# Three GpSimd products of the SSD scan issued on VectorE, in a hybrid SSD and S5 decoder step

## The chip, the cores and the metric

The kernel runs on one core of a Trainium2 chip. The metric is the device time of one execution in microseconds. The kernel before takes 1764.91 us (median of three runs, 1763.91 to 1765.38). In the names below, TensorE is PE, VectorE is DVE, ScalarE is ACT, GpSimd is POOL, and SyncE, whose queue issues all transfers here, is SP.

## The reference

One layer with two token mixers works on 1024 prompt tokens and on 64 tokens of 8 sample sequences, 1088 in all. One projection of the normed input (w_in, 1024 to 10272 columns) gives the columns of both mixers. The part that the change touches is the first mixer, a Mamba-2 scan in chunks of 128 tokens, with 32 heads of 64 columns in 8 groups of 4 heads:

```python
X = x.astype(jnp.float32) * dt[..., None]
dA = dt * A
A_cs = jnp.cumsum(dA, axis=-1)
Lmat = jnp.exp(jnp.where(causal, A_cs[..., :, None] - A_cs[..., None, :], -jnp.inf))
CB = jnp.einsum('bclgn,bcsgn->bgcls', Cc, Bc)
Y_diag = jnp.einsum('bgcls,bgrcls,bcsgrp->bclgrp', CB, Lmat, X)
decay_states = jnp.exp(A_cs[..., -1:] - A_cs)
states = jnp.einsum('bclgn,bgrcl,bclgrp->bcgrpn', Bc, decay_states, X)
...
Y_off = jnp.einsum('bclgn,bcgrpn,bgrcl->bclgrp', Cc, new_states[:, :-1], jnp.exp(A_cs))
Y = Y_diag + Y_off
```

So a chunk needs X (x times dt), X times decay_states for the state that it adds, and C times exp(A_cs) for what it takes from the state before it.

## The kernel before

Weights stand on TensorE as the fixed operand, and tokens stream. A product in float32 is made of three: the weight tile is split into a rounded part, `whi` (ACT, L143), and a rest, `wlo` (DVE, L144), the input is split likewise (`hh`, `hl`), and `dense` (L146) issues for each of 8 slices whi by hh, wlo by hh, whi by hl. A weight tile of 128 columns is used in three blocks of 512, 288 and 288 tokens, that is 24 matmuls each. `raw`, `whi` and `wlo` have two buffers each, so a tile can be split while the tile before it is in use.

The scan runs in eight stages, one for each group of heads. A main stream issues the tiles of group g+1 (`conv_tile`: three tap products on DVE at L591, a tanh on ACT at L592, L593 on DVE; `gate_tile`: tanh L606, product L607), and `drive` (L161) lets a side stream, `ssd` of group g, step in after each block; the table BESIDE says how many steps stand behind each block. `ssd` first handles the sample tokens (chunk 8) and then, for c from 0 to 7, `prepare(c+1)` and `outputs(c)`.

`prepare` loads the cumulated decays (`bca`, an SP transfer, two buffers), has PE transpose x and B into PSUM (`pst`), and then makes: the mask (`msk`: L671 on DVE, four exponentials on ACT at L673, L682 on DVE), B's split (`b`, `bt`), `xdt` (x times dt, DVE from PSUM, L679), `xd` (xdt times the decay, POOL, L681), C times exp(A_cs) in place of `bca` (exponential on ACT at L684, product on POOL at L685), and the split of `xd` (rounded part by ACT at L688, rest `xl` on POOL at L689). `outputs` multiplies msk by xdt and bca by the state `st` into `psy`, DVE writes the sum with the skip term from it (`ysb`, L743), PE makes the chunk's state in `pss`, and DVE forms the new state: the old one times the chunk's decay (L752), plus `pss` (L753). `st` is needed by the next chunk's matmuls.

Engines run their own instructions in order. The framework's scheduler sets the order on DVE, ACT, POOL and SP when the program is built; on PE the order is that in which the code issues the matmuls (class `Ordered`). `decays` (L483) makes the factors for all chunks once, ahead of the stages: `dt`, `dec` and others, each a tile of 9 times 32 columns.

Of the kernel before, what the change touches and what calls it, by code (L numbers as in the profile page):

```python
# [12 lines left out]
F32 = mybir.dt.float32  # L13
# [4 lines left out]
MUL, ADD, SUB, MAX, MIN = ALU.mult, ALU.add, ALU.subtract, ALU.max, ALU.min  # L18

P = 128  # L20
# [53 lines left out]
class Kernel:  # L74
# [408 lines left out]
    def decays(self, p):  # L483

        nc, pk, cn = self.nc, self.pk, self.cn
        V, S = nc.vector, nc.scalar
# [32 lines left out]
        ea = self.t(p, [P, 256], "xdt", 2)[:, :32]  # L519
# [41 lines left out]
        V.tensor_tensor(self.dec[:64, 256:], tots[:64, :32], self.ncs[:64, 256:], op=ADD)  # L561
        S.activation(self.dec[:, :256], self.dec[:, :256], AF.Exp)
        S.activation(self.dec[:64, 256:], self.dec[:64, 256:], AF.Exp)
        ts = self.psum("s")
        self.mm(ts[:, :256], self.ones[:64], dab.rearrange("p b h -> p (b h)"), start=True, stop=True)
        S.activation(self.etots, ts[:, :256], AF.Exp)
# [65 lines left out]
    def ssd(self, p, g, xcs, szs):  # L632

        nc, a = self.nc, self.a
        V, S, G = nc.vector, nc.scalar, nc.gpsimd
# [8 lines left out]
        h4 = lambda x: x.rearrange("p (h q) -> p h q", h=4)  # L644
# [4 lines left out]
        def prepare(c):  # L649
            smp = c == 8  # L650
            L = 64 if smp else P
            hc = c * 32 + 4 * g
            cl = slice(c * P, c * P + L)
            ea = self.t(p, [P, 4, L], "bca", 2)
            nc.sync.dma_start(ea, self.d["cs"][4 * g:4 * g + 4, cl].partition_broadcast(P))
            if smp:
                xs = []
                for src in (x0, x1, Bc, Cc):
                    d = self.t(p, [P, 64], "xsm", 4)
                    G.tensor_copy(d.rearrange("p (b t) -> p b t", t=8),  # L660
                                  src[:, 1027:].rearrange("p (b t) -> p b t", t=11)[:, :, :8])
                    xs.append(d)
            else:
                xs = [s[:, cl] for s in (x0, x1, Bc, Cc)]
            pt = self.psum("t")
            for j in range(3):
                self.tr(pt[:L, j * P:(j + 1) * P], xs[j], self.ident)
            self.mm(pt[:L, 384:384 + L], xs[2], xs[3], start=True, stop=True)
            m = self.t(p, [P, 4, L], "msk", 2)
            ng = self.cn[:64, C_SNEG:C_SNEG + 64] if smp else self.neg  # L670
            V.tensor_tensor(m[:L], ea[:L], ng.unsqueeze(1).to_broadcast([L, 4, L]), op=ADD)  # L671
            for h in range(4):
                S.activation(m[:L, h], m[:L, h], AF.Exp, bias=self.ncs[:L, hc + h:hc + h + 1])  # L673
            bt = None if smp else (self.t(p, [P, P], "b3", 2, F32R), self.t(p, [P, P], "bt", 2, F32R))
            if not smp:
                S.copy(bt[0], pt[:, 256:384])
                V.tensor_tensor(bt[1], pt[:, 256:384], bt[0].bitcast(F32), op=SUB)
            xdt = self.t(p, [P, 256], "xdt", 2)
            V.tensor_tensor(h4(xdt[:L]), h4(pt[:L, :256]), self.dt[:L, hc:hc + 4].unsqueeze(2).to_broadcast([L, 4, 64]), op=MUL)  # L679
            xd = self.t(p, [P, 256], "xd", 1)  # L680
            G.tensor_tensor(h4(xd[:L]), h4(xdt[:L]), self.dec[:L, hc:hc + 4].unsqueeze(2).to_broadcast([L, 4, 64]), op=MUL)  # L681
            V.tensor_tensor(m[:L], m[:L], pt[:L, 384:384 + L].unsqueeze(1).to_broadcast([L, 4, L]), op=MUL)  # L682
            if 0 < c < 8:
                S.activation(ea, ea, AF.Exp)  # L684
                G.tensor_tensor(ea, ea, xs[3].unsqueeze(1).to_broadcast([P, 4, L]), op=MUL)  # L685
            if not smp:
                xh, xl = self.t(p, [P, 256], "x3", 2, F32R), self.t(p, [P, 256], "xl", 2, F32R)
                S.copy(xh, xd)  # L688
                G.tensor_tensor(xl, xd, xh.bitcast(F32), op=SUB)  # L689
                xd = xh, xl  # L690
            bx = smp and [stack(h, pt[:, 256:384], xd) for h in range(2)]
            chunk[c] = (L, hc, cl, xs, ea, m, bt, xdt, xd, bx)

        def stack(h, bs, xd):


            own, other, last = (slice(32 * q, 32 * q + 32) for q in (h, 1 - h, 2))
            b3, x3 = self.t(p, [P, P], "b3", 2, F32R)[:96], self.t(p, [P, 256], "x3", 2, F32R)[:96]
            S.copy(b3[own], bs[own])
            S.copy(b3[last], bs[own])  # L700
            V.tensor_tensor(b3[other], bs[own], b3[own].bitcast(F32), op=SUB)
            S.copy(x3[own], xd[own])
            S.copy(x3[other], xd[own])
            V.tensor_tensor(x3[last], xd[own], x3[own].bitcast(F32), op=SUB)
            bx = self.t(p, [96, 4, P], "bx", 2, F32R)
            V.tensor_tensor(bx, b3.bitcast(F32).unsqueeze(1).to_broadcast([96, 4, P]),
                            self.cn[:96, C_S3:C_S3 + 4].unsqueeze(2).to_broadcast([96, 4, P]), op=MUL)
            return bx, x3
# [50 lines left out]
        def round_(r):  # L759
            bx, x3 = chunk[8][-1][r]  # L760
            for tag, b in ((("s", 0), ("t", 2)), (("y", 0), ("y", 2)))[r]:
# [4 lines left out]
                V.tensor_tensor(sv, sv, sp, op=ADD)  # L766

        prepare(8)
        yield
        past = earlier()  # L770
# [9 lines left out]
        nc.sync.dma_start(a["ssm_s"][g], s0)  # L780
        self.s0 = load(g + 1) if g < 7 else None
        prepare(0)
        yield
        for c in range(8):
            if c < 7:
                prepare(c + 1)
                yield
            outputs(c)
            yield
# [771 lines left out]
```

## Time and profile before

| | |
|---|---|
| median of three runs | 1764.91 us (1763.91 to 1765.38) |
| the profiled execution | 1763.57 us |
| its span, first to last instruction | 1761.4 us |
| mean granted TensorE clock | 0.994 |
| busy: PE, DVE, ACT, POOL | 1719.2, 1176.7, 685.4, 425.1 us |
| the eight scan stages | about 474 to 1215 us of the span |

A row of a timeline has the start in us, the length in us, the engine, the line, the operation, the tile written and the tiles read with buffer numbers left out, and in brackets how long the engine stood idle before it and for whom it waited. Instructions of one engine overlap a little: the next may start up to 0.09 us before the end that is recorded for the one ahead of it. A row of windows has, for a stretch of time, the busy time of each engine with the number of instructions in brackets, and then the clock that TensorE was granted.

### The profile page before, as it was taken

What the parts mean: (1) busy time and instruction counts of PE and PEld (TensorE: products, weight loads), DVE (VectorE), ACT (ScalarE), POOL (GpSimd) and SP (SyncE); (2) the same over time, 40 slices, a digit from 0 to 9 for tenths busy, and PEclk for the clock granted to TensorE, in tenths of its full rate; (3) what the DMA queues carried; (4) which work ended last, traced back from release to release, by engine and by line L of the source; (5) the groups of instructions that cost most, each with busy time, mean ns of one, the idle gap of its engine ahead of it and who ended that gap; (6) DMA issues with size and microseconds to landing.
All of it is one profiled execution on the core that took longest, in us unless ns stands there. A gap on an engine that the chain in (4) does not pass through costs nothing.

```text
span 1761.4 us, 31495 instructions
## 1 busy us (share of the span) xinstructions
PE 1719.2 (98%) x12510; PEld 1559.5 (89%) x12510; DVE 1176.7 (67%) x1976; ACT 685.4 (39%) x1414; POOL 425.1 (24%) x588
## 2 busy tenths in 40 slices
PE   9999999999999999999999999999999999999996
PEld 8997888889888888888878888888899989999996
DVE  6899977636586777778676877754565723485444
ACT  6422222223354544545444445445632302242221
POOL 0013212100143333424243333332341000022014
PEclk9999999999999999999999999999999999999998
DMA  5334343442132223232332222334523855474522
GB/s 209 96 103 117 103 152 106 126 143 76 54 105 91 91 79 121 62 126 61 87 107 80 100 89 96 108 117 147 165 98 122 259 175 195 132 226 137 197 97 75
DMA packets 138690, 212.62 MB, mean 121 GB/s; under 512 B 14832, under 2 KB 95120, under 8 KB 136496
## 3 DMA queue, kind: packets, MB, share of 16 engines
q1 hardware_dynamic: 138544, 210.62, 37.3%
q8 instruction: 98, 1.61, 0.4%
q14 instruction: 48, 0.39, 0.1%
HBM read 158.55 MB, written 52.03 MB: 120 GB/s over the span
## 4 chain that ended last, share of the span: by engine, by line
PE 70%; DVE 14%; DMA 5%; ACT 5%; issue 3%; POOL 2%; SPq 0%; POOLq 0%; ACTq 0%; DVEq 0%
PE psd L61 59%; PE psy L61 5%; PE pst L61 4%; DVE xc L591 4%; DMA bca<-d_cs 2%; PE pss L61 2%; POOL xd L681 2%; DMA yz<-d_yz 1%; ACT xp L592 1%; DVE xc L593 1%; DVE wlo L144 1%; DVE msk L671 1%; ACT msk L673 1%; DVE hl L61 1%; DVE cm L61 1%
## 5 line engine op out<-in xcount | busy, mean ns | idle before, releaser
L61 PE MATMUL psd<-hh,whi 128*128 128x512 f32 (+2 forms) x1872 | 619.9, 331 | 1.7 <-ACT zt L627 1.5
L61 PE MATMUL psd<-hh,wlo 128*128 128x512 f32 (+2 forms) x1872 | 608.0, 325 | 0.0
L61 PE MATMUL psd<-hl,whi 128*128 128x512 f32 (+2 forms) x1872 | 608.0, 325 | 0.0
L61 PEld LDWEIGHTS psd<-hh,whi 128*128 128x128 f32 x1872 | 352.7, 188 | 37.1 <-issue 9.4
L61 PEld LDWEIGHTS psd<-hl,whi 128*128 128x128 f32 x1872 | 352.3, 188 | 23.9
L61 PEld LDWEIGHTS psd<-hh,wlo 128*128 128x128 f32 x1872 | 352.8, 188 | 21.5
L144 DVE TENSOR_TENSOR wlo<-raw,whi 128x1024 fp32r<-128x1024 f32 (+1 forms) x139 | 171.7, 1236 | 149.8 <-ACT whi L143 149.6
L143 ACT CAST whi<-raw 128x1024 fp32r<-128x1024 f32 (+1 forms) x139 | 144.8, 1043 | 166.4 <-PE psd L61 106.4
L591 DVE SCALAR_TENSOR_TENSOR xc<-xp,pk,xc 128x1112 f32<-128x1112 f32 x96 | 149.6, 1558 | 20.3 <-ACT xc L589 19.0
L61 PE MATMUL psd<-ynh,whi 128*128 128x272 f32 x512 | 148.6, 290 | 0.0
L61 PE MATMUL psd<-ynl,whi 128*128 128x272 f32 x512 | 147.7, 288 | 0.0
L61 PE MATMUL psd<-ynh,wlo 128*128 128x272 f32 x512 | 147.3, 288 | 0.0
L673 ACT ACTIVATE msk<-msk,ncs 128x128 f32<-128x128 f32 (+1 forms) x288 | 93.3, 387 | 125.4 <-DVE msk L671 122.0
L685 POOL TENSOR_TENSOR bca<-bca,xc 128x512 f32<-128x512 f32 x56 | 85.0, 1518 | 130.4 <-ACT bca L684 121.4
L1325 POOL TENSOR_TENSOR fs<-fs,zt 128x272 f32<-128x272 f32 x24 | 26.2, 1090 | 336.6 <-ACT zt L1323 239.9
L61 PEld LDWEIGHTS psd<-ynh,whi 128*128 128x128 f32 x512 | 96.4, 188 | 0.3
L61 PEld LDWEIGHTS psd<-ynh,wlo 128*128 128x128 f32 x512 | 96.3, 188 | 0.1
L61 PEld LDWEIGHTS psd<-ynl,whi 128*128 128x128 f32 x512 | 96.2, 188 | 0.0
L681 POOL TENSOR_TENSOR xd<-xdt,dec 128x256 f32<-128x256 f32 (+1 forms) x72 | 58.4, 812 | 143.5 <-DVE xdt L679 105.3
L671 DVE TENSOR_TENSOR msk<-bca,cn 128x512 f32<-128x512 f32 (+1 forms) x72 | 53.6, 745 | 43.7 <-DMA bca<-d_cs 43.3
L61 PE MATMUL psd<-mh,wlo 128*128 128x272 f32 x256 | 73.8, 288 | 0.0
L61 PE MATMUL psd<-ml,whi 128*128 128x272 f32 x256 | 73.8, 288 | 0.0
(372 smaller groups left out, 3224.2 us busy)
## 6 DMA issues: line engine op xcount, KB each, us to landing
raw<-wt SPq DMA_DIRECT2D x143, 512.0 KB, 3.9
bca<-d_cs SPq DMA_DIRECT2D x64, 256.0 KB, 3.5
d_yz<-ysb SPq DMA_DIRECT2D x16, 544.0 KB, 3.4
yz<-d_yz SPq DMA_DIRECT2D x32, 272.0 KB, 4.5
s<-s SPq DMA_DIRECT2D x8, 1024.0 KB, 4.8
ssm_s<-s SPq DMA_DIRECT2D x8, 1024.0 KB
x<-xt SPq DMA_DIRECT2D x16, 272.0 KB, 5.6
d_ud<-ub SPq DMA_DIRECT2D x8, 544.0 KB, 3.6
```

The costliest lines, as they stand in the source:

```text
L61: ins = f(*args, **kw).ins
L143: S.copy(hi, raw)
L144: V.tensor_tensor(lo, raw, hi.bitcast(F32), op=SUB)
L591: V.scalar_tensor_tensor(xc[:, :W], xp[:, j:j + W], cw(j), xc[:, :W], op0=MUL, op1=ADD)
L592: S.activation(xp[:, :W], xc[:, :W], AF.Tanh)
L593: V.scalar_tensor_tensor(xc[:, :W], xp[:, :W], 1.0, xc[:, :W], op0=ADD, op1=MUL)
L671: V.tensor_tensor(m[:L], ea[:L], ng.unsqueeze(1).to_broadcast([L, 4, L]), op=ADD)
L673: S.activation(m[:L, h], m[:L, h], AF.Exp, bias=self.ncs[:L, hc + h:hc + h + 1])
L681: G.tensor_tensor(h4(xd[:L]), h4(xdt[:L]), self.dec[:L, hc:hc + 4].unsqueeze(2).to_broadcast([L, 4, 64]), op=MUL)
L685: G.tensor_tensor(ea, ea, xs[3].unsqueeze(1).to_broadcast([P, 4, L]), op=MUL)
L1325: G.tensor_tensor(total[q], total[q], sq[:, :nb], op=ADD)
```

## The change

The products at L681, L685 and L689 are issued on VectorE. `xd` is made straight from the transposes in PSUM by a factor `dec` times `dt`, which `decays` now makes for all chunks with two products. Nothing else is edited; behind L563 line numbers grow by two.

```diff
         S.activation(self.dec[:, :256], self.dec[:, :256], AF.Exp)
         S.activation(self.dec[:64, 256:], self.dec[:64, 256:], AF.Exp)
+        V.tensor_tensor(self.dec[:, :256], self.dec[:, :256], self.dt[:, :256], op=MUL)
+        V.tensor_tensor(self.dec[:64, 256:], self.dec[:64, 256:], self.dt[:64, 256:], op=MUL)
         ts = self.psum("s")
...
             xd = self.t(p, [P, 256], "xd", 1)
-            G.tensor_tensor(h4(xd[:L]), h4(xdt[:L]), self.dec[:L, hc:hc + 4].unsqueeze(2).to_broadcast([L, 4, 64]), op=MUL)
+            V.tensor_tensor(h4(xd[:L]), h4(pt[:L, :256]), self.dec[:L, hc:hc + 4].unsqueeze(2).to_broadcast([L, 4, 64]), op=MUL)
             V.tensor_tensor(m[:L], m[:L], pt[:L, 384:384 + L].unsqueeze(1).to_broadcast([L, 4, L]), op=MUL)
             if 0 < c < 8:
                 S.activation(ea, ea, AF.Exp)
-                G.tensor_tensor(ea, ea, xs[3].unsqueeze(1).to_broadcast([P, 4, L]), op=MUL)
+                V.tensor_tensor(ea, ea, xs[3].unsqueeze(1).to_broadcast([P, 4, L]), op=MUL)
             if not smp:
                 xh, xl = self.t(p, [P, 256], "x3", 2, F32R), self.t(p, [P, 256], "xl", 2, F32R)
                 S.copy(xh, xd)
-                G.tensor_tensor(xl, xd, xh.bitcast(F32), op=SUB)
+                V.tensor_tensor(xl, xd, xh.bitcast(F32), op=SUB)
                 xd = xh, xl
```

The order on PE stays what it was. The scheduler gives DVE, ACT and SP another order. Three places matter below, all in the stage of the fourth group (760 to 856 us of the trace); the other stages from the second to the seventh have the same rows there. Numbers behind a tile's name tell buffers apart.

The first place is TensorE's own order around chunk 6's outputs, shown of the changed program. psy_9435 and psy_9441 are the two halves of chunk 6's outputs, pss_9447 is its state, and psd_9461 is the first block of the second gate tile, with the weights whi_9456 and wlo_9457.

```order
L61 MATMUL psy_9441<-msk_9311,xdt_9321 64x128 x2
L61 MATMUL psy_9441<-bca_9304,st_9348 64x128 x2
L61 MATMUL pss_9447<-x_1598_9328,b_1594_9317 128x256
L61 MATMUL pss_9447<-x_1598_9328,bt_9318 128x256
L61 MATMUL pss_9447<-xl_9329,b_1594_9317 128x256
L61 MATMUL psd_9461<-hh_3_148,whi_9456 128x512
L61 MATMUL psd_9461<-hh_3_148,wlo_9457 128x512
```

Nothing moved here: the program before has the same rows, with buffer numbers two lower.

The second place is where VectorE makes the rest of that weight tile. Before, this is wlo_9455, and it stands behind chunk 4's ysb and st (psy_9248, psy_9254 and pss_9260 are chunk 4's):

```order
L743 SCALAR_TENSOR_TENSOR ysb_8552<-xc_7625,pk_70,psy_9248 128x128
L743 SCALAR_TENSOR_TENSOR ysb_8553<-xc_7783,pk_70,psy_9254 128x128
L753 TENSOR_TENSOR st_9264<-st_9264,pss_9260 128x256
L144 TENSOR_TENSOR wlo_9455<-raw_9453,whi_9454 128x1024
L682 TENSOR_TENSOR msk_9191<-msk_9191,pst_9186 128x512
```

Now it is wlo_9457, and it stands behind the ysb of both halves of chunk 6 (psy_9435, psy_9441) and behind chunk 7's mask, bca and xl:

```order
L745 SCALAR_TENSOR_TENSOR ysb_8554<-xc_7627,pk_70,psy_9435 128x128
L745 SCALAR_TENSOR_TENSOR ysb_8555<-xc_7785,pk_70,psy_9441 128x128
L684 TENSOR_TENSOR msk_9386<-msk_9386,pst_9381 128x512
L687 TENSOR_TENSOR bca_9379<-bca_9379,xc_8190 128x512
L691 TENSOR_TENSOR xl_9404<-xd_9398,x_1613_9403 128x256
L609 SCALAR_TENSOR_TENSOR sz_9269<-zt_9432,psd_9407 128x288
L754 TENSOR_TENSOR st_9451<-st_9348,etot_4711 128x256
L144 TENSOR_TENSOR wlo_9457<-raw_9455,whi_9456 128x1024
```

The split of the second gate tile's weights moved from two chunks ahead of its use to behind the last instruction that waits for chunk 6's outputs, which PE makes right before that use.

The third place, on VectorE too, is the state that chunk 4's outputs read (st_9181 before, with chunk 3's pss_9177; msk_9191 is chunk 5's mask, which needs a transfer into bca_9184). Before:

```order
L753 TENSOR_TENSOR st_9181<-st_9181,pss_9177 128x256
L677 TENSOR_TENSOR bt_9198<-pst_9186,b_1573_9197 128x128
L679 TENSOR_TENSOR xdt_9201<-pst_9186,dt_4708 128x256
L752 TENSOR_TENSOR st_9264<-st_9181,etot_4711 128x256
L671 TENSOR_TENSOR msk_9191<-bca_9184,cn_69 128x512
```

Now:

```order
L687 TENSOR_TENSOR bca_9139<-bca_9139,xc_8190 128x512
L691 TENSOR_TENSOR xl_9164<-xd_9158,x_1564_9163 128x256
L754 TENSOR_TENSOR st_9183<-st_9110,etot_4711 128x256
L673 TENSOR_TENSOR msk_9193<-bca_9186,cn_69 128x512
L755 TENSOR_TENSOR st_9183<-st_9183,pss_9179 128x256
```

The first step of chunk 5's mask, which waits for a transfer, moved ahead of the state's last step.

## The prediction

> **What bounds the kernel now.** I read the page's totals first, then the waits of TensorE, then the scan stages, then the timelines of one of them.
>
> ```profile
> span 1761.4 us, 31495 instructions
> PE 1719.2 (98%) x12510; PEld 1559.5 (89%) x12510; DVE 1176.7 (67%) x1976; ACT 685.4 (39%) x1414; POOL 425.1 (24%) x588
> ```
>
> TensorE is busy for all but 42 us of the span. A change that leaves its matmuls alone can win only what TensorE waits, or add to it. So each edit has one question: which wait of TensorE does it end or begin? The waits of TensorE in the scan stages (waiting line, waited for, us in total, times, longest):
>
> ```profile
> PE psy L61 <- DVE st L753: 8.5, 8, 2.2
> PE psy L61 <- DVE st L750: 3.7, 6, 1.4
> PE psy L61 <- DVE ysb L743: 2.6, 6, 1.2
> ...
> PE psy L61 <- POOL bca L685: 0.4, 1, 0.4
> PE pss L61 <- POOL xl L689: 0.2, 1, 0.2
> ```
>
> TensorE waits 14.8 us for three VectorE results and 0.6 us for GpSimd. The products that leave GpSimd are thus not what TensorE waits for; taking them off GpSimd is worth 0.6 us at that place. What counts is VectorE's queue. One whole stage in the view by windows:
>
> ```profile
> 760.40:855.60 95.20, 93.26 (x678) 82.06 (x677) 72.69 (x109) 46.58 (x106) 35.07 (x46) 1.00 0.28 93
> ```
>
> VectorE is busy for 72.7 of 95.2 us here. It is not full, but its results come in the order of its queue, and TensorE has only 1.9 us of idle time in a stage.
>
> **VectorE's load.** The first four rows are groups of instructions in the scan stages, the others are single lines with least, median and longest time in ns:
>
> ```profile
> L591 DVE SCALAR_TENSOR_TENSOR xc<-xp,pk,xc 128x1112 f32<-128x1112 f32 x84 | 133.1, 1584 | 19.9 <-ACT xc L589 19.0
> L752 DVE TENSOR_TENSOR st<-st,etot 128x256 f32<-128x256 f32 x56 | 31.9, 570 | 0.4
> L679 DVE TENSOR_TENSOR xdt<-pst,dt 128x256 f32<-128x256 f32 x64 | 26.4, 413 | 0.0
> ```
>
> ```profile
> L591 DVE SCALAR_TENSOR_TENSOR xc<-xp,pk,xc x96: 1360/1377/2298, 404.9 to 1118.6; 128x1112 f32<-128x1112 f32 x96
> L671 DVE TENSOR_TENSOR msk<-bca,cn x72: 406/690/1811, 457.0 to 1208.8; 128x512 f32<-128x512 f32 x64, 64x256 f32<-64x256 f32 x8
> L752 DVE TENSOR_TENSOR st<-st,etot x56: 406/452/1539, 501.6 to 1212.7; 128x256 f32<-128x256 f32 x56
> L704 DVE TENSOR_TENSOR x<-xd,x x16: 417/1522/2666, 476.7 to 1151.1; 32x256 fp32r<-32x256 f32 x16
> L144 DVE TENSOR_TENSOR wlo<-raw,whi x139: 420/1225/1635, 94.8 to 1733.3; 128x1024 fp32r<-128x1024 f32 x137, 128x256 fp32r<-128x256 f32 x1, 128x768 fp32r<-128x768 f32 x1
> L607 DVE SCALAR_TENSOR_TENSOR sz<-zt,psd x48: 440/455/690, 446.7 to 1139.3; 128x288 f32<-128x288 f32 x32, 128x512 f32<-128x512 f32 x16
> ```
>
> None of the three products has been on VectorE, so each is priced by the nearest row. xd, 256 columns from PSUM times a broadcast factor, is L679's form: 72 times 0.413, 29.7 us. The bca product, 512 columns from SBUF, is L671's: 56 times 0.69, 38.6 us. xl, 256 columns from SBUF, lies between L679's 0.413 and L704's least, 0.417: 64 times 0.417, 26.7 us. Together 95 us. Against that, VectorE's own instructions are longer in the mean than in the median: L591 by 133.1 - 84 x 1.377 = 17.4 us, L752 by 31.9 - 56 x 0.452 = 6.6 us. I take it that these 24 us go, since the long ones lie beside GpSimd's products of two operands; the bounds are 0 and 24. VectorE gains 71 to 95 us over eight stages, 9 to 12 in a stage, and stands at 82 to 85 of 95 us. It does not become the bound by its sum. The two products in `decays` (about 0.7 us) run once, with no matmul waiting for them until the first stage.
>
> **What becomes faster.** One wait shows why st is late now. The rows are those of ScalarE, then VectorE, then TensorE, around chunk 3's outputs:
>
> ```profile
> 809.67 0.41 ACT L688 CAST x<-xd 128x256 fp32r<-128x256 f32 x1 [3.95 <-POOL xd L681]
> ...
> 810.46 1.13 ACT L592 ACTIVATE xp<-xc 128x1112 f32<-128x1112 f32 x1
> ```
>
> ```profile
> 809.08 0.68 DVE L682 TENSOR_TENSOR msk<-msk,pst 128x512 f32<-128x512 f32 x1
> 809.68 0.59 DVE L743 SCALAR_TENSOR_TENSOR ysb<-xc,pk,psy 128x128 f32<-128x128 f32 x2
> 811.62 1.32 DVE L593 SCALAR_TENSOR_TENSOR xc<-xp,xc 128x1112 f32<-128x1112 f32 x1 [1.35 <-ACT xp L592]
> 812.86 0.41 DVE L753 TENSOR_TENSOR st<-st,pss 128x256 f32<-128x256 f32 x1
> ```
>
> ```profile
> 813.42 0.44 PE L61 MATMUL psy<-bca,st 128*64 128x128 f32 x4 [1.16 <-DVE st L753]
> ```
>
> ScalarE stands for GpSimd's xd, so its tanh (L592) is late, so VectorE stands 1.35 us, and st, next in its queue, keeps TensorE for 1.16 us. With xd on VectorE this chain is cut. The same relief serves the wait behind chunk 0 (L750) and the one for ysb. Of the 14.8 us, the longest wait for ysb lies in the first stage, behind the same tap products and tanh, with more ahead of it in the new order; I let it stay:
>
> ```profile
> 545.44 0.44 PE L61 MATMUL psy<-msk,xdt 128*64 128x128 f32 x4 [1.19 <-DVE ysb L743]
> ```
>
> That leaves 13.6 us; I take 12, because VectorE is fuller, with 8 and 16 as the ends (16 if each of the 20 waits hides another 0.13 us of restart).
>
> **What becomes slower: the weights' rest.** This is the second place of the order. TensorE needs wlo of the second gate tile right behind chunk 6's outputs:
>
> ```profile
> 835.96 0.42 PE L61 MATMUL psy<-bca,st 128*64 128x128 f32 x4
> ...
> 836.77 0.39 PE L61 MATMUL psd<-hh,whi 128*128 128x512 f32 x1
> 837.00 0.39 PE L61 MATMUL psd<-hh,wlo 128*128 128x512 f32 x1
> ```
>
> ```profile
> 821.90 1.23 DVE L144 TENSOR_TENSOR wlo<-raw,whi 128x1024 fp32r<-128x1024 f32 x1 [0.39 <-ACT whi L143]
> ```
>
> Now wlo is ready at 823.13, 13.9 us ahead of its first use at 837.00. In the new order it is the eighth of a run that begins with chunk 6's ysb. The second ysb can't start before psy is done (836.38 by these times), and wlo stands six instructions behind it. By the rows above: ysb 0.33, msk 0.68, bca 0.69, xl 0.42, sz 0.44, st 0.45, wlo 1.23, together 4.24 us. The next of a queue starts about 0.08 before the recorded end (809.08 + 0.68 against 809.68), six times: 3.76. From VectorE's end to TensorE's start lie 0.15 us (812.86 + 0.41 against 813.42): 3.9 us from psy's end to the first wlo matmul. It used to be 0.62. So TensorE stands 3.3 us more, and nothing hides it: its own queue is in order, and behind the first whi matmul all of its work needs wlo or comes later. It can't be under about 3.1, unless the run gets shorter; it is more, up to 4.2, where the mask's exponentials on ScalarE, the rounding of xd or VectorE's own backlog are late. The order has this run in six stages, the second to the seventh: 6 x 3.3 = 19.8 us, bounds 18.6 and 25.
>
> **The clock behind that wait.** Gaps before a TensorE instruction, and the clock granted in the 3.41 us from the places where it drops:
>
> ```profile
> 136.12 1.10 PE L61 MATMUL pst<-CA,bd 128*32 128x128 f32 x14 [2.74 <-DVE CA L1031]
> ```
>
> ```profile
> 499.03 0.66 PE L61 MATMUL psy<-msk,xdt 128*64 128x128 f32 x8 [1.93 <-DVE msk L682]
> ```
>
> ```profile
> 910.65 0.44 PE L61 MATMUL psy<-bca,st 128*64 128x128 f32 x4 [2.19 <-DVE st L753]
> ```
>
> ```profile
> 1415.40 0.47 PE L61 MATMUL psd<-gh,whi 128*128 128x512 f32 x1 [2.17 <-DVE zt L1200]
> ```
>
> ```profile
> 136.14:139.55 3.41, 3.40 (x23) 2.58 (x24) 3.39 (x8) 0.74 (x2) 1.64 (x3) 0.50 0.11 34
> 499.03:502.44 3.41, 3.25 (x20) 2.53 (x21) 3.23 (x8) 1.88 (x5) 2.35 (x4) 1.00 0.52 139
> 910.97:914.38 3.41, 3.41 (x22) 3.08 (x18) 3.33 (x9) 2.52 (x8) 1.08 (x2) 0.50 0.23 42
> ...
> 1416.14:1419.55 3.41, 3.41 (x9) 2.63 (x8) 1.59 (x2) 0.00 (x0) 0.00 (x0) 0.50 0.40 101
> ```
>
> Gaps of 2.17, 2.19 and 2.74 us are each followed by 3.41 us at half clock, which costs 1.7 us of matmul time; 1.93 is not. The drops lie 774.83 and 505.17 us apart, 227 and 148 times 3.413, so the clock is decided in fixed slots of 3.41 us, and the three gaps lie each in one slot. The new gap runs from the end of the whi matmul, 0.39 after 836.77, to 840.3: 3.1 us. At least 2.17 of it fall in one slot if it begins in the first 1.24 or the last 0.93 of a slot: 64%. So I count four of six: 4 x 1.7 = 6.8 us, bounds 0 and 10.2. The wait of 2.19 us, and its half clock, go with st's: -1.7. The Trainium skill (page TensorE: Matmul & The Clock Gate, section What's actually happening) says that the clock halves after an idle window of about 3.4 us; by that a gap of 3.1 us would leave it alone, and this term would be 0. The trace differs, with 2.17 us.
>
> **A smaller new wait** is the third place. Chunk 5's first mask step waits for a transfer into the buffer that chunk 3's outputs free, and now st for chunk 4's outputs stands behind it:
>
> ```profile
> 813.87 0.42 PE L61 MATMUL psy<-bca,st 128*64 128x128 f32 x4
> ```
>
> ```profile
> 818.80 0.39 PE L61 MATMUL psy<-bca,st 128*64 128x128 f32 x4
> ```
>
> ```profile
> bca<-d_cs SPq DMA_DIRECT2D x64, 256.0 KB, 3.5
> ```
>
> From chunk 3's end, 814.29, TensorE takes 4.5 us to the matmuls that read st. The new chain takes 3.5 for the transfer, 0.6 for the mask step, 0.41 and 0.15 for st: 4.7 us. That is 0.2 us in six stages, 1.2 us; bounds 0 and 3.
>
> **The sum**: +19.8 + 6.8 + 1.2 - 12 - 1.7 = +14.1 us on the profiled execution's 1763.57, which lies 1.3 below the median of the runs. On the median 1764.91: 1779.0 us.
>
> **The rivals.** First, the gap comes but the clock holds, as the 499.03 row allows: 14.1 - 6.8 = +7.3, 1772.2 us. For it speaks that only three gaps show the drop. Second, faster: the waits for st, chunk 0's state and ysb go whole with their restarts and the half clock (16 + 1.7), and VectorE's run to wlo is short. Its place is the same second gate tile. It ends faster by over 0.2% (3.5 us, about what a measurement of this kernel can tell from no change) only when the wait for wlo is under (17.7 - 1.2 - 3.5) / 6 = 2.2 us and the clock holds; at 1.5 us it is +9 + 1.2 - 17.7 = -7.5, 1757 us. Against it: six instructions and their 3.8 us have no short cut in the rows. Third, VectorE falls behind through the stage, msk and ysb come late too: waits for wlo of 4.2 (25), six half clocks (10.2), 3 at the third place, and only 8 won: +30 with no half clock saved, 1795 us. That GpSimd keeps the products can't be: the order has them on VectorE.
>
> **How the numbers follow.** The forecast has 0.65, the clock rival 0.15, the third 0.07, the faster one 0.07, and 0.06 is left for gains and losses that cancel. Range: from 1768, the clock rival with 16 won instead of 12 (1768.2), to 1791, the forecast with waits of 4.2 (+5.4) and six half clocks (+3.4) and 9 won (+3), which is 1790.8. Slower by over 0.2%: 0.65 + 0.15 + 0.07 less 0.01 for the low edge of the clock rival = 0.86; within: 0.07; faster: 0.07.
>
> **What would show it.** Right: the waits of TensorE have a new row, psd for wlo L144, six times about 3 us, the waits for st fall below 5 us, VectorE's busy time rises from 1177 to between 1248 and 1272 us, and stretches at half clock stand behind most of the six gaps. Wrong: no wait for wlo, or one below 2 us; or many waits for st beside it.

## The result, and the profile after

The changed kernel takes 1783.42 us (median of four runs, 1780.75 to 1787.18), the kernel before on the same chip 1764.41 (four runs, 1760.68 to 1765.38). The ratio is 1.0108, with a 95% interval from 1.0082 to 1.0134: slower by 19 us, where 14 were forecast. The profiled execution took 1781.98 us, with a mean granted clock of 0.985.

The totals of the profile after:

```profile
span 1780.2 us, 31288 instructions
PE 1727.5 (97%) x12510; PEld 1565.4 (88%) x12510; DVE 1219.2 (68%) x2170; ACT 688.7 (39%) x1414; POOL 233.9 (13%) x396
```

The span is 18.8 us longer. TensorE issues the same 12510 matmuls, yet is busy 8.3 us longer: that is the clock, which fell in the mean from 0.994 to 0.985. The other 10.5 us are idle time. The waits of TensorE in the scan stages of the kernel after, which answer to the first list of the prediction:

```profile
PE psd L61 <- DVE wlo L144: 19.1, 6, 3.7
PE psy L61 <- DVE msk L684: 1.6, 1, 1.6
PE psy L61 <- DVE ysb L745: 1.5, 1, 1.5
PE psy L61 <- DVE st L755: 1.1, 1, 1.1
PE psy L61 <- ACT b L678: 0.4, 1, 0.4
```

Twenty waits for st and ysb, 14.8 us, have become two of 2.6 us: -12.2. Six waits for the rest of a weight tile, wlo, 19.1 us, are new. All other rows of the list of TensorE's waits, over the whole program, are 3.3 us more together. Two of them make most of it:

```profile
PE psd L61 <- DVE zt L1202: 3.7, 2, 2.5
PE psd L61 <- ACT zt L629: 2.8, 1, 2.8
```

They were 2.4 and 1.5 us before. So 19.1 - 12.2 + 3.3 + 8.3 = 18.5 of the 18.8 us are accounted for.

The timeline of VectorE, then that of TensorE, at the third of the six new waits:

```profile
837.17 0.78 DVE L745 SCALAR_TENSOR_TENSOR ysb<-xc,pk,psy 128x128 f32<-128x128 f32 x2 [0.30 <-PE psy L61]
837.87 0.68 DVE L684 TENSOR_TENSOR msk<-msk,pst 128x512 f32<-128x512 f32 x1
838.47 0.68 DVE L687 TENSOR_TENSOR bca<-bca,xc 128x512 f32<-128x512 f32 x1
839.07 0.42 DVE L691 TENSOR_TENSOR xl<-xd,x 128x256 fp32r<-128x256 f32 x1
839.41 0.45 DVE L609 SCALAR_TENSOR_TENSOR sz<-zt,psd 128x288 f32<-128x288 f32 x1
839.77 0.42 DVE L754 TENSOR_TENSOR st<-st,etot 128x256 f32<-128x256 f32 x1
840.11 1.22 DVE L144 TENSOR_TENSOR wlo<-raw,whi 128x1024 fp32r<-128x1024 f32 x1
```

```profile
837.17 0.39 PE L61 MATMUL psy<-bca,st 128*64 128x128 f32 x4
...
837.95 0.39 PE L61 MATMUL psd<-hh,whi 128*128 128x512 f32 x1
841.38 0.80 PE L61 MATMUL psd<-hh,wlo 128*128 128x512 f32 x1 [3.04 <-DVE wlo L144]
```

The run stands as the order had it. VectorE begins ysb 0.30 us after it was free, for TensorE's psy, and from there it has no pause until wlo is made at 841.33; TensorE's first product with wlo starts 0.05 us later. That product takes 0.80 us where its like took 0.39 before. The windows of the 3.41-us slots around this wait, and around the fifth one (1040.01), have the clock as the third number from the right:

```profile
837.17:840.58 3.41, 1.17 (x12) 0.68 (x8) 3.32 (x8) 2.20 (x5) 0.00 (x0) 1.00 0.16 38
840.58:843.99 3.41, 2.61 (x6) 2.13 (x7) 2.87 (x5) 0.45 (x2) 0.00 (x0) 0.50 0.46 149
843.99:847.41 3.42, 3.42 (x9) 2.65 (x9) 0.00 (x0) 0.62 (x3) 0.00 (x0) 0.50 0.50 163
1038.55:1041.96 3.41, 1.95 (x9) 1.62 (x10) 3.41 (x6) 0.00 (x0) 0.00 (x0) 1.00 0.32 75
1041.96:1045.37 3.41, 3.41 (x17) 2.83 (x16) 0.12 (x1) 1.07 (x4) 0.00 (x0) 1.00 0.69 242
```

Behind the third wait two slots run at half clock; behind the fifth none does: its gap is cut by the border at 1038.55 into 1.58 and 1.46 us. Five of the six waits are followed by half clock. Between 200 and 1700 us the kernel after has nine slots at half clock, the one before two.

### The profile page after: what moved, and what is told of

Same layout as the page of the kernel before. It is cut to its first block, busy times and chain, and to the rows that moved or that the text cites. A ratio compares the mean times of both kernels' runs of the same rounds, so it can differ in the third digit from the quotient of the medians.

```text
span 1780.2 us, 31288 instructions
## 1 busy us (share of the span) xinstructions
PE 1727.5 (97%) x12510; PEld 1565.4 (88%) x12510; DVE 1219.2 (68%) x2170; ACT 688.7 (39%) x1414; POOL 233.9 (13%) x396
## 3 DMA queue, kind: packets, MB, share of 16 engines
q8 instruction: 98, 1.61, 0.4%
## 4 chain that ended last, share of the span: by engine, by line
PE 81%; DVE 11%; DMA 4%; ACT 2%; issue 1%; POOL 0%; SPq 0%; POOLq 0%; DVEq 0%; ACTq 0%
PE psd L61 68%; PE psy L61 6%; PE pst L61 4%; PE pss L61 3%; DMA bca<-d_cs 2%; DMA yz<-d_yz 1%; DVE xc L593 1%; DVE wlo L144 1%; DVE cm L61 1%; DVE hl L61 1%; DMA d_mb<-zt 1%; ACT yg L1167 1%; DVE msk L684 1%; DVE x L61 1%; ACT msk L675 0%
## 5 line engine op out<-in xcount | busy, mean ns | idle before, releaser
L61 PE MATMUL psd<-hh,wlo 128*128 128x512 f32 (+2 forms) x1872 | 614.4, 328 | 19.1 <-DVE wlo L144 19.1
L593 DVE SCALAR_TENSOR_TENSOR xc<-xp,pk,xc 128x1112 f32<-128x1112 f32 x96 | 131.7, 1372 | 2.3 <-ACT xc L591 1.5
L745 DVE SCALAR_TENSOR_TENSOR ysb<-xc,pk,psy 128x128 f32<-128x128 f32 x128 | 40.3, 344 | 58.3 <-PE psy L61 57.7
L673 DVE TENSOR_TENSOR msk<-bca,cn 128x512 f32<-128x512 f32 (+1 forms) x72 | 47.5, 659 | 40.2 <-DMA bca<-d_cs 39.8
L61 PE MATMUL psd<-mh,whi 128*128 128x272 f32 x256 | 73.8, 288 | 0.0
```

What stands on the lines that cost most here:

```text
L61: ins = f(*args, **kw).ins
L593: V.scalar_tensor_tensor(xc[:, :W], xp[:, j:j + W], cw(j), xc[:, :W], op0=MUL, op1=ADD)
L745: V.scalar_tensor_tensor(ys[q][:, cl], xs[q], self.pk[:, K_DS + 2 * g + q:K_DS + 2 * g + q + 1], yp[:, :L], op0=MUL, op1=ADD)
```

## The experiments

Three theories were put against each other. Theory 1 is the prediction's: the products themselves win their 12 us, and the price is the late wlo with the half clock behind it. Theory 2: the price is VectorE's greater load, and the late wlo is only where it shows first. Theory 3: the wait counts, the clock does not. Theories 1 and 2 take other forms in the later runs, as each expectation says. All ratios are against the kernel before, timed on the same chip.

### Taking the wait away, in two ways

The low products last: TensorE makes the 16 products with whi first, in the first block of the second gate tile. VectorE's order stays.

```diff
+            if last and bi == 0:
+                order = [(wh, m, k) for k in range(n) for m in (xh, xl)] + [(wl, xh, k) for k in range(n)]
...
-        yield from self.dense(idx, self.hh, self.hl, evac)
+        yield from self.dense(idx, self.hh, self.hl, evac, last=idx % 6 == 5)
```

> The changed kernel, with one edit: in the first block of every second gate tile TensorE makes the 16 products of the high weight half first and the 8 of the low half last. VectorE's order is untouched. Theory 1 (the price of the change is the late low half of the second gate tile's weights, 19.1 us of waits in six stages, and the half clock behind them, some 8 us): 16 products at 0.23 us cover 3.6 us, the waits are 3.0 to 3.7, so `psd<-hh,wlo` falls from 19.1 us to under 2, the half-clock stretches behind it go, and what remains is the gain at st and ysb: 1783 - 18 - 8 = about 1757, 1752 to 1761, faster than the kernel before (1764). Theory 2 (the greater load of VectorE, +42 us, is what costs; the low half is only where it shows first): the wait comes back at the next thing that TensorE wants from VectorE (ysb, st, the mask), and the time stays at 1777 to 1785. Theory 3 (the wait matters, the clock does not): 1764 to 1766.

Measured: 1749.68 us (1748.16 to 1754.70), ratio 0.9921 (0.9908 to 0.9934). Theory 1 holds, though the time lies 2 us below its range: 34 us were won against the change, not 26. The totals and one wait of this kernel:

```profile
PE 1717.7 (98%) x12510; PEld 1558.9 (89%) x12510; DVE 1217.9 (70%) x2170; ACT 688.9 (39%) x1414; POOL 234.1 (13%) x396
```

```profile
PE psd L61 <- DVE wlo L144: 0.3, 1, 0.3
```

The wait is gone, and nothing has come in its place with VectorE as busy as in the changed kernel (1217.9 against 1219.2 us). Theory 2 falls. Of the 32.1 us of span, 18.8 are the wait, 9.8 TensorE's busy time, and 3.5 waits elsewhere.

The weights earlier: the tile is asked for one tile ahead, so VectorE makes wlo before the chunk's products. AHEAD is 0, the first block.

```diff
+            if idx % 6 == 4 and bi == AHEAD:
+                self.ahead = self.weights(idx + 1)
-        yield from self.dense(idx, self.hh, self.hl, evac)
+        yield from self.dense(idx, self.hh, self.hl, evac, w=self.ahead if idx % 6 == 5 else None)
```

> The changed kernel, with the weights of every second gate tile asked for one tile ahead, behind the first block of the first gate tile: its low half then stands in VectorE's queue ahead of the chunk's products, not behind them. The same number of instructions on every engine. Theory 1 (late low half and half clock): the 19.1 us go and nothing else comes, 1752 to 1761, the same as with the low products last. Theory 2 (VectorE's load): the subtraction of 1.2 us per stage pushes the chunk's own products back by that much, and ysb, st or the mask is waited for in its place: 1775 to 1785. Theory 3 (wait without clock): 1764 to 1766.

Measured: 1748.27 us (1747.14 to 1752.82), ratio 0.9912 (0.9900 to 0.9924). No row for wlo is left among the waits, and those for st and ysb in the scan are 1.3 us together. The time is again below theory 1's range, by 4 us. It is the same gain by another way, so it is the wait that counts and not the order of the products.

The control is the order of the products in the kernel before:

> The kernel before, with the same order of the products (low half last in the first block of every second gate tile): the control. In the kernel before no low half of a second gate tile is waited for in stages two to seven, so theories 1, 2 and 3 all expect no change: 1762 to 1767. Were it faster by what theory 1 expects of the changed kernel (7 us or more), the order of the products would be worth something by itself, and the gain of that run could not be put down to the late low half.

Measured: 1763.15 us (1758.45 to 1768.47), ratio 1.0001 (0.9990 to 1.0012). That order is worth nothing where wlo is not late.

### The clock by itself

```diff
+            for _ in range(FILL if fill and bi == 0 else 0):
+                self.mm(ps[:, :nb], wh[:, 0], xh[0][:, b0:b0 + nb], start=True, stop=True)
```

FILL is 12. The edit reaches seven stages, not the six of the expectation: in the one where wlo is not late it adds 2.7 us of work.

> The changed kernel, with the first product of the second gate tile's first block made 12 times more in stages two to seven, thrown away by the real one that starts the sum anew: 12 x 0.23 = 2.7 us of work in the 3.04 us in which TensorE waits for the low half, which still comes when it comes. The wait in the list of waits falls to 0.3 to 1.0 us each. Theory 1 (wait 19.1, half clock 8, both count): the half clock behind the six waits goes and the wait itself stays, hidden in work that nobody needs: 1783 - 8 = 1775, 1772 to 1778. Theory 3 (the clock does not count): no change, 1782 to 1785. Theory 2 (VectorE's load): also no change, 1780 to 1785.

Measured: 1773.63 us (1771.13 to 1778.31), ratio 1.0055 (1.0043 to 1.0067). The 84 needless matmuls make the kernel 10 us faster than the changed one. Its totals and its wait for wlo:

```profile
PE 1735.5 (98%) x12594; PEld 1571.8 (89%) x12594; DVE 1219.0 (69%) x2170; ACT 689.5 (39%) x1414; POOL 233.3 (13%) x396
```

```profile
PE psd L62 <- DVE wlo L145: 2.7, 6, 1.0
```

Of the 19.1 us of waits 16.4 are filled, and the fillers are 84 x 0.227 = 19.1 us; but TensorE is busy only 8.0 us longer than in the changed kernel. The difference, 11 us, goes to the clock: between 200 and 1700 us one slot at half clock is left of nine, and none in the scan. Two of the eight that went lay at the end of the scan and behind it, so not all of the 11 us belong to the six waits. Theory 3 falls.

### The wait without the products

The kernel before, with wlo of the second gate tile held behind the chunk's second ysb:

```diff
-                self.split([x[:, part] for x in (hi, lo, raw)], nc.scalar, nc.vector)
+                ins = self.split([x[:, part] for x in (hi, lo, raw)], nc.scalar, nc.vector)
+                if idx % 6 == 5 and 6 < idx < 48:
+                    self.tc.add_manual_dep(ins, self.behind.name, NOSYNC, reason="order")
...
```

(`self.behind` is the last ysb instruction; `split` now returns the instruction that makes wlo.)

> The kernel before, no product moved; only the low half of the second gate tile's weights is held back on VectorE behind the chunk's second ysb, in seven stages. The order then has it directly behind the st product that waits for the state matmuls, two matmuls ahead of its use, as the run with the decayed x and C's product had it for the first gate tile (gaps of 2.25 to 2.5 us, one of 3.6). Theory 1 (the late low half and the half clock behind it are the price of the change): 7 x 2.4 = 17 us of waits, and four half clocks of 1.7 us, 1763 + 17 + 7 = about 1787, 1779 to 1795, with VectorE's busy time unchanged at 1177 us. Theory 2 (the price is VectorE's load): no change or under 5 us, 1762 to 1768.

Measured: 1799.91 us (1797.52 to 1801.33), ratio 1.0211 (1.0191 to 1.0231). The totals and the waits in the scan:

```profile
PE 1733.4 (96%) x12510; PEld 1568.9 (87%) x12510; DVE 1175.7 (65%) x1976; ACT 686.4 (38%) x1414; POOL 424.3 (24%) x588
```

```profile
PE psd L61 <- DVE wlo L146: 25.9, 7, 4.2
PE psy L61 <- DVE st L755: 8.1, 7, 2.0
PE psy L61 <- DVE st L752: 2.8, 5, 1.5
```

With VectorE's load unchanged the order alone costs 38 us: 25.9 of waits and 14.2 of TensorE's busy time, less the 3.0 that ysb and st wait less. The direction is that of theory 1; its size was too low by 13, because six of the gaps are 3.3 to 4.2 us and not 2.4. One of them shows why:

```profile
853.30 0.69 DVE L684 TENSOR_TENSOR msk<-msk,pst 128x512 f32<-128x512 f32 x1 [0.48 <-ACT msk L675]
854.42 0.45 DVE L609 SCALAR_TENSOR_TENSOR sz<-zt,psd 128x288 f32<-128x288 f32 x1 [0.44 <-ACT zt L608]
854.79 0.60 DVE L745 SCALAR_TENSOR_TENSOR ysb<-xc,pk,psy 128x128 f32<-128x128 f32 x2
855.31 0.41 DVE L755 TENSOR_TENSOR st<-st,pss 128x256 f32<-128x256 f32 x1
855.64 1.26 DVE L146 TENSOR_TENSOR wlo<-raw,whi 128x1024 fp32r<-128x1024 f32 x1
```

Ahead of ysb VectorE stands twice for ScalarE, for the mask's exponentials and for the gate's tanh. So what stands ahead of wlo in VectorE's queue sets the price, and it can be worse than in the changed kernel.

### The three products apart

Each of these is the kernel before with some of the three products on VectorE. Theory 1 took it that GpSimd's decayed x, xd, holds ScalarE up; the rival that the products win together. The decayed x alone:

```diff
+        V.tensor_tensor(self.dec[:, :256], self.dec[:, :256], self.dt[:, :256], op=MUL)
...
-            G.tensor_tensor(h4(xd[:L]), h4(xdt[:L]), self.dec[:L, hc:hc + 4].unsqueeze(2).to_broadcast([L, 4, 64]), op=MUL)
+            V.tensor_tensor(h4(xd[:L]), h4(pt[:L, :256]), self.dec[:L, hc:hc + 4].unsqueeze(2).to_broadcast([L, 4, 64]), op=MUL)
```

> The kernel before, with only the decayed x moved (straight from the transposes, one factor for all chunks); the other two products stay on GpSimd. VectorE gets 72 products of 0.41 us instead of 192. In its order no low half of a gate tile stands behind the chunk's outputs. Theory 1 (the 12 us at st and ysb come from cutting GpSimd's xd out of ScalarE's way, and the price comes only from the late low half): the whole gain without the price, waits for st and ysb down from 14.8 to under 5 us, time 1749 to 1757. Theory 2 (the products buy their gain together, each by taking work away from beside VectorE's instructions): a third of it, 1758 to 1762.

Measured: 1745.18 us (1742.92 to 1748.19), ratio 0.9899 (0.9885 to 0.9912). This is the lowest time of all, 1.0% below the kernel before and 4 us below theory 1's range, with 1198.3 us of VectorE. The whole gain comes without the price: of the 17.6 us of span, 11.6 are the waits for st and ysb (14.8 to 3.2), 4.7 TensorE's busy time.

The other two products, without it:

```diff
-                G.tensor_tensor(ea, ea, xs[3].unsqueeze(1).to_broadcast([P, 4, L]), op=MUL)
+                V.tensor_tensor(ea, ea, xs[3].unsqueeze(1).to_broadcast([P, 4, L]), op=MUL)
...
-                G.tensor_tensor(xl, xd, xh.bitcast(F32), op=SUB)
+                V.tensor_tensor(xl, xd, xh.bitcast(F32), op=SUB)
```

> The kernel before, with only C's product (bca) and the rest of the decayed x (xl) moved; the decayed x itself stays on GpSimd, ahead of ScalarE's rounding and tanh. No low half is late in the order. Theory 1 (xd is what keeps ScalarE): most of the waits for st and ysb stay, 10 us or more of 14.8, time 1759 to 1765; less than that only in so far as GpSimd's xd starts earlier when it has no other work ahead of it. Theory 2 (shared relief): two thirds of the gain, 1752 to 1757.

Measured: 1749.43 us (1748.39 to 1752.55), ratio 0.9927 (0.9915 to 0.9940). Both expectations fail: the time is below either range, nearer to theory 2's. Theory 1 in its narrow form falls: the decayed x need not leave GpSimd. But the gains do not add up either: 18 us for xd and 14 for the other two.

C's product (bca) alone, and the rest (xl) alone, each by its one line of the diff above:

> The kernel before, with only C's product (bca) moved to VectorE. Theory 1 in the form that the run of C's product and the rest together calls for (the decayed x need not leave GpSimd; it has to stop standing in GpSimd's queue behind products that themselves wait for ScalarE: C's product waits 121 us for its exponential in the scan): ScalarE's wait for the decayed x falls from 103 us to under 75, the waits for st and ysb from 14.8 to under 8, 1747 to 1756. If the decayed x itself has to go: 1759 to 1765. If the gain is shared by the products: 1757 to 1761.

Measured: 1749.88 us (1749.06 to 1754.34), ratio 0.9934 (0.9917 to 0.9951).

> The kernel before, with only the rest of the decayed x (xl) moved to VectorE. It waits only 25.8 us in GpSimd's queue, but 0.84 us of it stand ahead of the next decayed x. Theory 1 in its wider form (GpSimd's queue ahead of the decayed x): less is won than with C's product, 1752 to 1761, with the waits for st and ysb in step with ScalarE's wait for the decayed x. If the decayed x itself has to go: 1759 to 1765. If the gain is shared by the products: 1757 to 1761.

Measured: 1766.52 us (1763.12 to 1769.46), ratio 1.0020 (1.0008 to 1.0032). C's product alone wins 12 us, as theory 1 in its second form expected; the rest alone wins nothing, it is 0.2% slower, and that is less than any of the three expected.

The decayed x on VectorE, and made once more by GpSimd for nobody:

```diff
+            if not smp:
+                xl = self.t(p, [P, 256], "xl", 2, F32R)
+                G.tensor_tensor(h4(xl[:L]), h4(xdt[:L]), self.dec[:L, hc:hc + 4].unsqueeze(2).to_broadcast([L, 4, 64]), op=MUL)
...
```

> The decayed x on VectorE as in the run with it alone, and GpSimd makes the same product all the same, from the tile xdt, into the tile that the rest xl later overwrites: nobody reads it. GpSimd is as loaded as in the kernel before. Theory 1 (what counts is when the decayed x reaches ScalarE's queue, whoever makes it): as with the decayed x alone (1745), 1742 to 1750, ScalarE's wait for it 40 to 55 us in the scan. Theory 2 (what counts is GpSimd's work beside VectorE's instructions): the gain goes again, 1757 to 1764.

Measured: 1747.95 us (1744.33 to 1749.74), ratio 0.9918 (0.9901 to 0.9935). GpSimd is as busy as in the kernel before (435.1 against 425.1 us), and the gain stays: the interval overlaps that of xd alone. ScalarE's wait for xd is 52.3 us, in the range that theory 1 gave. So theory 2 falls here: giving GpSimd this work back does not take the gain away.

Where no wlo is late, the gain goes with ScalarE's wait for the decayed x in the scan stages, though not in proportion. One row each: the kernel before, the rest alone, C's product alone, the decayed x alone:

```profile
ACT x L688 <- POOL xd L681: 102.9, 49, 4.0
```

```profile
ACT x L688 <- POOL xd L681: 99.0, 44, 3.7
```

```profile
ACT x L688 <- POOL xd L681: 70.8, 35, 3.4
```

```profile
ACT x L690 <- DVE xd L683: 45.8, 32, 3.0
```

At 103 and 99 us nothing is won; at 71 and 46 the waits of TensorE for st and ysb are 5.3 and 3.2 us, and the gain is there. With bca and xl moved it is 64.7 us and they are 5.3; in the changed kernel 23.5 and 2.6. So below about 70 us little more is won, which would be why the gains do not add; why it is so no run shows. In the run with the rest alone the waits for st are still there, eleven of them (11.9 us) named after a GpSimd copy that ends last. One stands behind chunk 3:

```profile
914.25 0.44 PE L61 MATMUL psy<-bca,st 128*64 128x128 f32 x4 [2.03 <-POOL xsm L660]
```

The instruction reads st, which VectorE ended at 914.10; all eleven waits end 0.15 us behind VectorE's st. With them st and ysb are waited for during 16.0 us in this run. GpSimd's rows, VectorE's, then ScalarE's ahead of it:

```profile
905.66 1.28 POOL L685 TENSOR_TENSOR bca<-bca,xc 128x512 f32<-128x512 f32 x1 [2.57 <-ACT bca L684]
908.60 1.61 POOL L681 TENSOR_TENSOR xd<-xdt,dec 128x256 f32<-128x256 f32 x1 [1.66 <-DVE xdt L679]
```

```profile
905.85 2.27 DVE L591 SCALAR_TENSOR_TENSOR xc<-xp,pk,xc 128x1112 f32<-128x1112 f32 x1
908.04 0.41 DVE L679 TENSOR_TENSOR xdt<-pst,dt 128x256 f32<-128x256 f32 x1
```

```profile
910.24 0.41 ACT L688 CAST x<-xd 128x256 fp32r<-128x256 f32 x1 [3.72 <-POOL xd L681]
```

The tap product L591 takes 2.27 us beside bca where its median is 1.38, so xdt is late by 0.9. Then xd itself takes 1.61 us, where 0.61 is usual, beside the next tap product (908.38 to 909.74). So in this place bca lengthens what goes ahead of xd rather than standing ahead of it in the queue. How much the one and the other give in the run with C's product alone isn't settled: that edit takes both away.

### Two products

> The kernel before, with the decayed x and its rest (xl) moved, C's product left on GpSimd. No low half is late in the order. Theory 1: as with the decayed x alone, 1749 to 1757, since VectorE has room for 27 us more. The theory that VectorE's load costs: 5 us or more slower than with the decayed x alone.

Measured: 1750.32 us (1749.84 to 1751.27), ratio 0.9927 (0.9914 to 0.9941). It lies in theory 1's range, but 5.1 us above the decayed x alone, as the load theory had it. The waits for st and ysb are 6.2 us, against 3.2 there, and between 200 and 1700 us one slot more is at half clock. So xl on VectorE has a price, some 3 us of waits here, where it takes 0.73 us with bca on GpSimd (64 in 46.5 us; 0.42 in the changed kernel). Whether that is the load or the new order isn't told apart. It isn't what made the change slower: with all three products and wlo in time, the kernel takes 1748 to 1750.

> The kernel before, with the decayed x and C's product moved, the rest (xl) left on GpSimd. Here VectorE's order puts the low half of the FIRST gate tile of a stage directly behind the st product that waits for the chunk's state matmuls, two matmuls ahead of its use, in six stages; none of a second gate tile is late. Theory 1 (a low half behind a product that waits for TensorE costs its chain): 0.41 + 1.23 + 0.3 of passing on - 0.39 = about 1.5 us six times, 9 us, too short for the half clock (1.93 us kept it, 2.17 did not), so 1752 + 9 = about 1761, 1757 to 1766, with a row `psd <- wlo` of six times 1.5 us. Theory 2 (load, not order): between the runs with one and with three products more, by the number of the products, so no slower than with the decayed x and its rest by more than 3 us, and no such row.

Measured: 1764.30 us (1760.95 to 1766.18), ratio 1.0006 (0.9997 to 1.0014). The other two pairs win, this one doesn't, and a row of its waits says why:

```profile
PE psd L61 <- DVE wlo L144: 15.6, 6, 3.6
```

The place is the one that the order shows, and theory 2 expected no such row. The six waits are 2.6 us and not 1.5, and three of them are followed by half clock. None was expected to be, by the row of 1.93 us that the prediction too had misread (below).

## Why the prediction was right

**The weights' rest** was taken at 6 x 3.3 = 19.8 us and is 19.1. The run of instructions, its start behind psy and the absence of cover are as written. In the rows above the first wlo matmul starts 3.43 us behind the whi matmul, and such matmuls follow each other by 0.23 otherwise: 3.20 us late, 0.1 less than forecast, because TensorE starts 0.05 us behind VectorE's end here and not 0.15. The list counts only 3.04 of it as a wait; the other 0.16 us is the end of the whi matmul, which the next one would have covered, and stands in the busy time.

**What becomes faster** was taken at -12, and is -12.2. The reason given for it was too narrow. The chain from xd over ScalarE to st is there, but moving xd is only one way of cutting it: taking C's product alone off GpSimd does nearly as much. That the size agrees to 0.2 us is in part luck: the 12 were a choice between 8 and 16, and the 1.19 us for ysb in the first stage, which were left standing, went, while one of 1.5 us for ysb came in the last stage.

**The clock** is the term that was mis-sized: +6.8 - 1.7 = +5.1 was forecast. TensorE is busy for 29.9 us in slots at half clock between 200 and 1700 us, against 6.8 before; by estimate half of that is lost, so the clock costs some 11.5 us more. The whole busy time grew by 8.3 only, since 14 waits fewer in the scan (10 against 24), at 0.16 us each, give back about 2. The step that failed is the limit of 2.17 us in one slot. It rested on the row at 499.03, a gap of 1.93 us that keeps the clock; but by the prediction's own slots a border lies at 497.96, 121 slots ahead of 910.97, and cuts that gap into 0.86 and 1.07 us. The runs put the limit near 1.85 (below). With it the same working gives 82%, five of six, and five of the six waits are followed by half clock, one of them by two slots. Two more slots came behind the longer waits for ysb (1.50 us at 1225) and for zt L629 (2.84 us), which the sum did not have. The run with the fillers is what shows that the clock has a price.

**VectorE's load.** The three products were priced at 29.7, 38.6 and 26.7 us. The groups in the scan stages, after:

```profile
L593 DVE SCALAR_TENSOR_TENSOR xc<-xp,pk,xc 128x1112 f32<-128x1112 f32 x84 | 115.2, 1372 | 2.0 <-ACT xc L591 1.5
L687 DVE TENSOR_TENSOR bca<-bca,xc 128x512 f32<-128x512 f32 x56 | 38.4, 686 | 0.5 <-ACT bca L686 0.5
L683 DVE TENSOR_TENSOR xd<-pst,dec 128x256 f32<-128x256 f32 (+1 forms) x72 | 29.9, 416 | 0.0
L691 DVE TENSOR_TENSOR xl<-xd,x 128x256 fp32r<-128x256 f32 x64 | 26.9, 420 | 0.5 <-ACT x L690 0.5
L754 DVE TENSOR_TENSOR st<-st,etot 128x256 f32<-128x256 f32 x56 | 23.5, 420 | 0.3
```

They are 29.9, 38.4 and 26.9, yet the busy time grew by 42.5 us and not by 71 to 95: this sign of being right did not come. The relief was undersized: L593 gave 17.9 us and L754 8.4, and besides the mask step (53.2 to 47.1), L595 (39.8 to 36.8) and wlo (60.0 to 57.4) gave 11.7; one row (x from xd and x, 24.6 to 29.2) took 4.6 back. The 19 us that are left lie in the overlap between neighbours in the queue: the recorded lengths of all of VectorE's instructions add up to 94.4 us more than its busy time before, and to 116.0 after, 21.6 more. That VectorE does not become the bound was right, and the low products last show it.

**The smaller new wait** (+1.2) can't be told apart: one wait for st of 1.1 us is left where six of 0.2 were expected. The waits elsewhere, the end of the scan and the tiles behind it above all, give 3.3 us that the sum left out.

The forecast of 1779.0 stands against 1783.42, 4.4 us low: 3.2 of TensorE's busy time and 3.3 of the waits elsewhere, less 0.7 at wlo, 0.2 at st and ysb and the 1.2 of the third place.

## What to carry to other kernels

When instructions move onto an engine with room to spare, look in its queue for the one that the busiest engine needs next, and ask what the new ones put ahead of it; the sum of busy times says nothing about that. Where such a wait appears, let the waiting engine do first what doesn't need the late result, or ask for it earlier: here either of these turned a loss of 19 us into a gain of 14 to 15. And move the parts one at a time: one of the three products, alone, gave the whole gain.

## What the runs showed of the hardware

**The clock's slots.** In the fourteen profiled executions the time between 100 and 1715 us was cut into slots of 3.413 us, laid by the places where the clock drops, and TensorE's idle time summed in each. In all 47 slots with 1.85 us or more of idle time the next slot ran at half clock; in the 19 with 1.5 to 1.85, in three; in the 20 with 1.3 to 1.5, in none. So it is idle time of about half a slot that counts, not the length of one gap. Behind a slot that itself ran at half clock (two of the 47 did) less is enough: of the 58 such slots, the 48 with 0.45 us or less of idle time were followed by full clock and the ten with 0.52 or more by half clock again. That is why the third wait cost two slots: the slot at 840.58 has 0.80 us of idle time. Two gaps of nearly equal length in the run with the weights earlier, and the clock of the slots behind:

```profile
499.95 1.04 PE L62 MATMUL psy<-msk,xdt 128*64 128x128 f32 x7 [2.04 <-DVE msk L687]
...
1401.42 0.47 PE L62 MATMUL psd<-gh,whi 128*128 128x512 f32 x1 [2.07 <-DVE zt L1205]
```

```profile
500.00:503.41 3.41, 3.41 (x15) 2.79 (x16) 3.41 (x11) 2.38 (x5) 0.37 (x2) 0.50 0.58 154
1397.71:1401.12 3.41, 1.63 (x13) 1.40 (x11) 1.61 (x3) 1.04 (x1) 0.00 (x0) 1.00 0.94 318
1401.12:1404.53 3.41, 3.11 (x14) 2.61 (x15) 2.10 (x4) 0.00 (x0) 0.00 (x0) 1.00 0.43 134
```

The first gap lies whole in the slot that ends at 500.00, and the clock halves; the second is cut by the border at 1401.12, 1.77 us on one side, and it holds. The slots don't start with the kernel: at the gap of 2.74 us near 136 us, which all fourteen have, the drop comes from 1.06 us ahead of the gap's end to 2.19 us behind it. So the same gaps meet the slots otherwise in each execution, and that may be one source of the spread of some microseconds between runs of one kernel; no run shows how much.

**GpSimd beside VectorE.** The tap product (L591) takes 1584 ns in the mean in the kernel before, and 1370 to 1372 in the runs without GpSimd's bca, with xd and xl still there or not; with bca still on GpSimd it is 1560 to 1589. In the kernel before the one that begins second is lengthened: the 20 tap products that begin while a bca runs take 2.20 to 2.30 us, the 22 during which a bca begins take 1.37 to 1.38 and leave bca with up to 2.22. So too with xd: the 13 that begin during a tap product take 1.61 us instead of 0.61, and the tap product keeps its 1.36 to 1.37. The product xdt, which reads one of its operands from PSUM, is 413 to 417 in the kernel before and in the changed one. The Trainium skill (page SBUF — State Buffer, section Who interferes with whom) says that a VectorE instruction with two SBUF inputs contends with a GpSimd instruction that reads SBUF, and that one with at most one such input, outside the modes that use two ports, does not. The trace agrees. The time of this kernel does not follow it, though: with xd alone on VectorE the mean is 1589, and that is the kernel with the lowest time.
